# When the summed weight blocks of a pair are formed, and where the fourth sum is put

## Chip, cores and metric

The kernel runs on one core of a Trainium2 chip, in float32. The metric is the device time of one execution in microseconds (us), as the median of several runs. PE is the matmul engine (TensorE), DVE is VectorE, ACT is ScalarE, POOL is GpSimd and SP is SyncE, which issues most DMAs here.

## What is computed

One layer of an encoder trunk for 512 tokens of width 1024:

```python
h = _rmsnorm(x, g_pre_mix)
q, k, v, g, u, sv, a_ret, a_sgu = jnp.split(h @ w_in, ...)
y_ret = _retention_branch(q, k, v, g, ret_decay_logit, w_ret_o)
y_sgu = _sgu_branch(u, sv, sgu_ln_g, sgu_ln_b, w_spatial, b_spatial, w_sgu_o)
merged = jax.nn.sigmoid(a_ret) * y_ret + jax.nn.sigmoid(a_sgu) * y_sgu
x = x + _rmsnorm(merged @ w_out, g_post_mix)
h2 = _rmsnorm(x, g_pre_ffn)
x = x + _rmsnorm(_conv_gated_mlp(h2, w_up, conv_w, conv_b, w_down), g_post_ffn)
```

Nearly all of the time goes into the matrix products with w_in, w_ret_o, w_sgu_o, w_out, w_up and w_down.

## The kernel before

Every float32 operand of a product is split in two parts, hi (rounded, by ACT, line 79) and lo (the rest, by DVE, line 86), and a product is three matmuls: hi by hi, hi by lo, lo by hi.

Part of the products is done by Strassen's scheme in Winograd's form, with seven block products in place of eight. In the projections of u, of the two gates and in most of the up projection, 256 output columns form a *pair* (in the up projection, where two neighbouring tiles of the hidden layer are paired, it is called a couple here). Its weights are four blocks B11, B12, B21, B22 of 128 x 512 each, which come in two loads: a holds B11 and B12, b holds B22 and B21. Seven weight blocks, the *forms*, are wanted in the order B11, B21, T1, T2, T3, T4, B22, where

```python
T1 = B11 + B12;  T2 = T1 + B22;  T3 = B12 + B22;  T4 = T2 + B21
```

There are 20 pairs: four for u, four for each of the two gates, eight couples in the up projection. In the gates and the up projection two ordinary blocks of 128 x 1024 (`w_block`) stand between the forms of a pair, one after T2 and one after B22.

`w_form` makes one form: where needed it loads or adds, and then it splits the block into a slot of tag w4 (nine slots), from which PE reads. `w_get` calls it some units ahead of PE's use. The loads and the sums lie in tiles of tag raw, of which there are four buffers; a pair needs three of them: a, b, and t for the sums. T1 and T3 are added by DVE (lines 167 and 168), T2 and T4 by POOL (lines 169 and 171). T3 overwrites B12 in a; T2 is in the second half of t, and T4 overwrites T2.

The products of a pair are in the class `Pair`. Three PSUM tiles are in use. The product of T2 is copied out by ACT (line 79, `c<-ps` in the up projection) before the product of T3 is accumulated on the same bank; that of T3 is copied out in the same way before the second product of the activations with T4; and DVE's subtraction in line 720 reads the bank of T1's product before that of B22 is accumulated on it. Ordinary products (`f_block`) stand between.

A scheduler puts the instructions of each engine into an order when the program is built. It goes by the order in the source, by the free buffers and by its own estimate of times, so an instruction that is issued earlier in the source can bring others to other places. Each engine then runs its own list strictly in that order and waits at the head of it for semaphores of the others. POOL's list also has the DMAs that POOL issues, among them four loads of xT (line 658) in the middle of the first pair.

Of the kernel before, what the change touches and what calls it, by code (L numbers as in the profile page):

```python
# [13 lines left out]
ALU = mybir.AluOpType  # L14
# [3 lines left out]
S = 512  # L18
# [29 lines left out]
def tile_block(ctx: ExitStack, tc, xT, x, wall, par, cs, wsp, bsp, gpost, gffn, out):  # L48
    nc = tc.nc
# [6 lines left out]
    def nm(s):  # L56
        uid[0] += 1
        return f"{s}_{uid[0]}"

    def blk(dt=F32, n="blk", shape=(P, S)):  # L60
        return sb.tile(list(shape), dt, tag="blk", bufs=NBLK, name=nm(n))

    def tmp(n="tmp", shape=(P, S)):
        return sb.tile(list(shape), F32, tag="tmp", bufs=6, name=nm(n))
# [19 lines left out]
    def split(hi, lo, src):  # L84
        copy(hi, src)
        nc.vector.tensor_sub(lo, src, as32(hi))  # L86
# [31 lines left out]
    w_ready, w_pos, w_held, w_raw = {}, [0, 0], [0], {}  # L118

    def raw_tile():  # L120
        return sb.tile([P, 1024], F32, tag="raw", bufs=4, name=nm("raw"))
# [4 lines left out]
    def slot(n, at=0, w=1024):  # L126
        return sb.tile([P, 1088], F32R, tag="w4", bufs=9, name=nm(n))[:, at : at + w]
# [28 lines left out]
    def w_form(form, i):  # L156

        if form == "B11":
            a, b = raw_tile(), raw_tile()
            nc.sync.dma_start(a, wall[i])  # L160
            nc.sync.dma_start(b, wall[i + 1])
            w_raw["B11"], w_raw["B12"] = a[:, :S], a[:, S:]
            w_raw["B22"], w_raw["B21"] = b[:, :S], b[:, S:]
        elif form == "T1":
            t = raw_tile()
            w_raw["T1"], w_raw["T2"], w_raw["T3"], w_raw["T4"] = t[:, :S], t[:, S:], w_raw["B12"], t[:, S:]
            nc.vector.tensor_add(w_raw["T1"], w_raw["B11"], w_raw["B12"])  # L167
            nc.vector.tensor_add(w_raw["T3"], w_raw["B12"], w_raw["B22"])
            nc.gpsimd.tensor_tensor(out=w_raw["T2"], in0=w_raw["T1"], in1=w_raw["B22"], op=ALU.add)  # L169
        elif form == "T4":  # L170
            nc.gpsimd.tensor_tensor(out=w_raw["T4"], in0=w_raw["T2"], in1=w_raw["B21"], op=ALU.add)
        w = slot("wf", 0, 1088)
        lo, hi = w[:, AT_64 : AT_64 + S], w[:, S + AT_192 : 2 * S + AT_192]
        split(hi, lo, w_raw[form])
        return hi, lo
# [21 lines left out]
    def w_unit(u):  # L197
        return w_block(u[1]) if u[0] == "blk" else (w_down if u[0] in "qt" else w_form)(*u)
# [93 lines left out]
    T0, T1 = slice(0, 256), slice(256, 512)  # L292
# [35 lines left out]
    for t in range(NT):  # L328
        for n in range(2):
# [3 lines left out]
                out=xt, in_=xt, func=AF.Square, accum_out=ss[:, 4 * n + t : 4 * n + t + 1]  # L333
# [19 lines left out]
    for c in range(19, 1, -2):  # L353
        v.scalar_tensor_tensor(
            out=lc, in0=lc, scalar=1.0 / c, in1=lb, op0=ALU.add, op1=ALU.mult
# [4 lines left out]
        out=lg, in0=lc, scalar=-2.0, in1=lg, op0=ALU.mult, op1=ALU.add  # L360
# [5 lines left out]
    for m in range(8):  # L366
        t = blk(n="qkraw")
# [286 lines left out]
    for n, acc in enumerate(t_group()):  # L654
        if n < 2:
            for k in (n + 2, n + 6):
                t = tmp("xT")
# [663 lines left out]
```

## Time and profile before

| | |
|---|---|
| time, median of 3 runs | 827.69 us (824.78 to 828.19) |
| the profiled execution: its own time / its span | 827.49 us / 825.7 us |
| PE busy | 815.4 us (99%) |
| DVE busy | 661.4 us (80%) |
| ACT busy | 440.8 us (53%) |
| POOL busy | 101.0 us (12%) |
| POOL's T2 (line 169) | 20 times, mean 1.809 us |
| POOL's T4 (line 171) | 20 times, mean 1.333 us |
| granted clock of PE | 0.999 |

All lines quoted from the profile are of one execution. Times in the timeline are in us from the start of the span; a row gives start, duration, engine, line, operation, written tile <- read tiles, shapes and count, and in brackets how long the engine had been idle before it and what ended that. Rows of the groups give busy time and the mean of one in ns, then the idle time before them. Rows of the waits give the waiting instruction, the one waited for, the total, the count and the longest. Matmuls are pipelined, so their rows overlap: what one costs is the distance of its start to the next one's.

### The profile page before, as it was taken

The page shows a single profiled execution, that of the slowest core. Times are in us where ns is not written, and L with a number is a line of the kernel's source. Part 1 is how long each engine was busy: PE and PEld are TensorE (multiplying, and loading weights), DVE is VectorE, ACT ScalarE, POOL GpSimd, SP SyncE. Part 2 cuts the span into 40 slices and gives each one's busy share as a digit, 9 for nine tenths or more (in the row PEclk, how much of TensorE's full clock was granted, in tenths as well). Part 3 has the DMA queues.
Part 4 walks back from the last instruction along what each step waited for, and adds up shares of the span by engine and source line. Part 5 has one row for each costly group of instructions (what it writes and reads, how often), then busy time and mean ns, then how long its engine had stood idle before and what let it go on. Part 6 is the DMA issues. An engine that isn't in the chain of part 4 may idle for free.

```text
span 825.7 us, 13263 instructions
## 1 busy us (share of the span) xinstructions
PE 815.4 (99%) x5152; PEld 735.0 (89%) x5152; DVE 661.4 (80%) x1101; ACT 440.8 (53%) x771; POOL 101.0 (12%) x102
## 2 busy tenths in 40 slices
PE   9999999999999999999999999999999999999996
PEld 7888888888899999999988898899999998999996
DVE  7489897878797777767765568979899899988967
ACT  6636445546665444444445685556566566544531
POOL 0010000102121111132211211210111200000001
PEclk9999999999999999999999999999999999999999
DMA  8733222212223232222349111322322341233244
GB/s 294 246 116 102 77 77 77 77 52 78 90 102 129 103 102 80 101 101 103 108 166 339 48 55 55 103 102 103 102 103 102 102 154 52 77 115 129 96 147 154
DMA packets 29215, 93.24 MB, mean 113 GB/s; under 512 B 3360, under 2 KB 4000, under 8 KB 29152
## 3 DMA queue, kind: packets, MB, share of 16 engines
q1 hardware_dynamic: 26928, 86.85, 30.2%
q0 software_dynamic: 1360, 4.46, 1.6%
q10 hardware_dynamic: 864, 1.09, 0.4%
q8 instruction: 40, 0.66, 0.3%
q14 instruction: 23, 0.19, 0.1%
HBM read 88.19 MB, written 4.19 MB: 112 GB/s over the span
## 4 chain that ended last, share of the span: by engine, by line
PE 91%; DVE 6%; ACT 1%; issue 1%; DMA 0%; POOL 0%; DVEq 0%; SPq 0%; POOLq 0%; ACTq 0%
PE ps L692 23%; PE ps L217 12%; PE ps L218 12%; PE ps L219 12%; PE ps L1058 8%; PE ps L481 5%; PE ps L480 5%; PE ps L482 5%; PE ps L836 2%; PE ps L837 2%; PE ps L838 2%; PE ps L1074 1%; PE ps L761 1%; DVE fl L86 1%; PE ps L279 1%
## 5 line engine op out<-in xcount | busy, mean ns | idle before, releaser
L86 DVE TENSOR_TENSOR wl<-raw,wh 128x1024 fp32r<-128x1024 f32 (+1 forms) x93 | 109.1, 1182 | 48.9 <-PE ps L692 24.2
L79 ACT ACTIVATE wf<-raw 128x512 fp32r<-128x512 f32 x140 | 85.3, 627 | 102.7 <-PE ps L218 34.0
L86 DVE TENSOR_TENSOR wf<-raw,wf 128x512 fp32r<-128x512 f32 x140 | 111.1, 808 | 23.3 <-ACT wf L79 22.4
L692 PE MATMUL ps<-sh,wf 128*128 128x256 f32 x640 | 119.5, 277 | 0.0
L79 ACT ACTIVATE wh<-raw 128x1024 fp32r<-128x1024 f32 (+2 forms) x95 | 93.3, 993 | 37.4 <-DMA raw<-wall 17.0
L692 PEld LDWEIGHTS ps<-sh,wf 128*128 128x128 f32 x640 | 101.1, 188 | 0.8 <-ACT u L79 0.2
L217 PE MATMUL ps<-h2h,wh 128*128 128x512 f32 (+1 forms) x256 | 92.4, 363 | 0.7 <-ACT h2h L906 0.7
L218 PE MATMUL ps<-h2l,wh 128*128 128x512 f32 (+1 forms) x256 | 92.4, 363 | 0.0
L219 PE MATMUL ps<-h2h,wl 128*128 128x512 f32 (+1 forms) x256 | 92.1, 361 | 0.0
L692 PE MATMUL ps<-sl,wf 128*128 128x256 f32 x320 | 88.8, 278 | 0.0
L480 PE MATMUL ps<-wh,xh 128*128 128x512 f32 x192 | 75.0, 391 | 0.0
L481 PE MATMUL ps<-wl,xh 128*128 128x512 f32 x192 | 74.9, 390 | 0.0
L482 PE MATMUL ps<-wh,xl 128*128 128x512 f32 x192 | 74.8, 390 | 0.0
L169 POOL TENSOR_TENSOR raw<-raw,raw 128x512 f32<-128x512 f32 x20 | 36.2, 1809 | 235.2 <-DVE raw L167 207.8
L1058 PE MATMUL ps<-dl,fh 128*128 128x256 f32 x216 | 60.8, 281 | 0.1
L1058 PE MATMUL ps<-dh,fl 128*128 128x256 f32 x216 | 60.7, 281 | 0.0
L1058 PE MATMUL ps<-dh,fh 128*128 128x256 f32 x216 | 60.7, 281 | 0.0
L692 PEld LDWEIGHTS ps<-sl,wf 128*128 128x128 f32 x320 | 60.0, 188 | 0.6
L219 PEld LDWEIGHTS ps<-h2h,wl 128*128 128x128 f32 x256 | 48.0, 188 | 7.7
L217 PEld LDWEIGHTS ps<-h2h,wh 128*128 128x128 f32 x256 | 47.9, 188 | 7.9 <-ACT h2h L906 1.0
L692 PE MATMUL ps<-xh,wf 128*128 128x256 f32 x288 | 54.2, 278 | 0.0
L218 PEld LDWEIGHTS ps<-h2l,wh 128*128 128x128 f32 x256 | 48.0, 188 | 6.6
(314 smaller groups left out, 2048.9 us busy)
## 6 DMA issues: line engine op xcount, KB each, us to landing
raw<-wall SPq DMA_DIRECT2D x145, 512.0 KB, 3.6
x<-x SPq DMA_DIRECT2D x24, 256.0 KB, 5.9
xT<-xT SPq DMA_DIRECT2D x8, 256.0 KB, 5.4
x<-x POOLq DMA_DIRECT2D x8, 256.0 KB, 2.4
xT<-xT POOLq DMA_DIRECT2D x4, 256.0 KB, 3.6
out<-zg SPq DMA_DIRECT2D x4, 256.0 KB, 2.0
out<-zs ACTq DMA_DIRECT2D x3, 256.0 KB, 3.5
cs<-cs SPq DMA_DIRECT2D x2, 256.0 KB, 4.1
```

The lines of the kernel that those rows point to most:

```text
L79: nc.scalar.activation(out=o, in_=i, func=AF.Copy)
L86: nc.vector.tensor_sub(lo, src, as32(hi))
L169: nc.gpsimd.tensor_tensor(out=w_raw["T2"], in0=w_raw["T1"], in1=w_raw["B22"], op=ALU.add)
L217: nc.tensor.matmul(o, ah, bh, start=start, stop=False)
L218: nc.tensor.matmul(o, ah, bl, start=False, stop=False)
L219: nc.tensor.matmul(o, al, bh, start=False, stop=stop)
L480: nc.tensor.matmul(acc[t], xh[k][:, c], wh[:, f], start=k == 0, stop=False)
L481: nc.tensor.matmul(acc[t], xh[k][:, c], wl[:, f], start=False, stop=False)
L482: nc.tensor.matmul(acc[t], xl[k][:, c], wh[:, f], start=False, stop=k == KD - 1)
L692: nc.tensor.matmul(o, w_[:, c], a_, start=first and k == n == 0, stop=k == 3 and n == 2, skip_group_check=True,)
L836: nc.tensor.matmul(o, ah, bh, start=k == 0, stop=False)
L1058: nc.tensor.matmul(o, a_[:, c], w_[:, f], start=j == t == i == 0, stop=j == DP - 1 and i == 2 and n not in (M2, M3, M4), skip_group_check= ...
```

## The change

T1 and T2 are made as part of the pair's first form (B11), right after its two loads are issued, and t is taken there. T3 is made when it is its turn. T4 is made with form T1, and written over B11, so it no longer has to wait for the split of T2; in place of that it may not be written before B11 has been split.

```diff
             w_raw["B11"], w_raw["B12"] = a[:, :S], a[:, S:]
             w_raw["B22"], w_raw["B21"] = b[:, :S], b[:, S:]
+            t = raw_tile()
+            w_raw["T1"], w_raw["T2"], w_raw["T3"], w_raw["T4"] = t[:, :S], t[:, S:], w_raw["B12"], w_raw["B11"]
+            nc.vector.tensor_add(w_raw["T1"], w_raw["B11"], w_raw["B12"])
+            nc.gpsimd.tensor_tensor(out=w_raw["T2"], in0=w_raw["T1"], in1=w_raw["B22"], op=ALU.add)
+        elif form == "T3":
+            nc.vector.tensor_add(w_raw["T3"], w_raw["B12"], w_raw["B22"])
         elif form == "T1":
-            t = raw_tile()
-            w_raw["T1"], w_raw["T2"], w_raw["T3"], w_raw["T4"] = t[:, :S], t[:, S:], w_raw["B12"], t[:, S:]
-            nc.vector.tensor_add(w_raw["T1"], w_raw["B11"], w_raw["B12"])
-            nc.vector.tensor_add(w_raw["T3"], w_raw["B12"], w_raw["B22"])
-            nc.gpsimd.tensor_tensor(out=w_raw["T2"], in0=w_raw["T1"], in1=w_raw["B22"], op=ALU.add)
-        elif form == "T4":
             nc.gpsimd.tensor_tensor(out=w_raw["T4"], in0=w_raw["T2"], in1=w_raw["B21"], op=ALU.add)
```

## The prediction

> **What bounds the kernel now.** I read the page first, for the engines' shares, then the stretches of 20 us, for where TensorE (PE) has any time free, then who waited for whom on PE.
>
> ```profile
> span 825.7 us, 13263 instructions
> PE 815.4 (99%) x5152; PEld 735.0 (89%) x5152; DVE 661.4 (80%) x1101; ACT 440.8 (53%) x771; POOL 101.0 (12%) x102
> 180.00:200.00 20.00, 19.73 (x95) 16.11 (x94) 15.25 (x27) 12.04 (x20) 5.28 (x7) 1.00 0.25 80
> 200.00:220.00 20.00, 19.72 (x111) 16.91 (x110) 16.73 (x26) 12.19 (x22) 3.79 (x3) 1.00 0.20 66
> 560.00:580.00 20.00, 20.00 (x131) 18.15 (x130) 19.35 (x31) 13.28 (x23) 2.94 (x2) 1.00 0.28 102
> PE ps L605 <- DVE o L615: 0.3, 1, 0.3
> PE ps L624 <- DVE o L615: 0.3, 1, 0.3
> ```
>
> The first two lines say that the span is PE's work: 815.4 of 825.7 us, so 10.3 us is all that PE leaves, ends included. The three stretches (columns: length, PE, its weight loads, DVE, ACT, POOL, clock, DMA) lie where the 20 pairs of weights are formed; PE is free for 0.27 and 0.28 us in the first two and not at all in the third. PE's waits in that part are the last two lines, and neither names a sum of weights. In the changed program PE's instructions come in the same order, one for one. So the change can give back at most some tenths of a microsecond, and it can cost only where it makes PE wait.
>
> **What leaves, comes and moves.** No arithmetic is added: per pair two adds on DVE (T1, T3) and two on GpSimd (POOL: T2, T4), as before; no DMA is added and SP's queue keeps its order. Lines are those of before: T1 L167, T3 L168, T2 L169, T4 L171.
>
> ```profile
> L169 POOL TENSOR_TENSOR raw<-raw,raw 128x512 f32<-128x512 f32 x20 | 36.2, 1809 | 235.2 <-DVE raw L167 207.8
> POOL raw L171 <- DVE wf L86: 71.4, 19, 14.1
> 571.83 1.29 DVE L86 TENSOR_TENSOR wf<-raw,wf 128x512 fp32r<-128x512 f32 x2
> 573.03 0.69 DVE L86 TENSOR_TENSOR fl<-gp,fh 128x512 fp32r<-128x512 f32 x1
> 573.64 0.68 DVE L167 TENSOR_TENSOR raw<-raw 128x512 f32<-128x512 f32 x1
> 574.36 0.69 DVE L168 TENSOR_TENSOR raw<-raw,raw 128x512 f32<-128x512 f32 x1
> 574.97 0.42 DVE L720 TENSOR_TENSOR c<-ps,c 128x256 f32<-128x256 f32 x1
> 575.30 2.28 DVE L86 TENSOR_TENSOR wf<-raw,wf 128x512 fp32r<-128x512 f32 x2
> 574.55 1.64 POOL L169 TENSOR_TENSOR raw<-raw,raw 128x512 f32<-128x512 f32 x1 [19.45 <-DVE raw L167]
> 577.66 1.30 POOL L171 TENSOR_TENSOR raw<-raw,raw 128x512 f32<-128x512 f32 x1 [1.47 <-DVE wf L86]
> ```
>
> *The wait of T4.* POOL's T4 waited 71.4 us in 19 pairs for T2's split on DVE. That wait goes: T4 now needs T2, which POOL itself has just made, and the splits of B11, which are two products older. It is off PE's path: POOL has 12% of the span to do. What becomes late next is nothing on POOL; T2 and T4 now run back to back, about 1.64 + 1.30 = 2.9 us.
>
> *What that does to DVE.* At 574.55 T2 runs on POOL; the splits that DVE starts at 575.30 take 2.28 us for two, where the two at 571.83 take 1.29: 1.0 us is lost while POOL works. L720 in between, with one input from PSUM, keeps its 0.42. So each POOL sum that falls into a dense run of DVE costs DVE about 1.0 us, and the T4 that used to run at 577.66 now falls into the same run as T2. The Trainium skill (SBUF — State Buffer, "Who interferes with whom") says that a VectorE instruction with two SBUF inputs and a GpSimd instruction that reads SBUF exclude each other for a whole instruction, whichever issued second waiting; the row agrees, and this rule speaks against putting T4 right behind T2.
>
> *Where it meets PE.* In three couples of the up projection (those at 571, 613 and 634 us) the changed program also sets other work back: ACT's copy of the product of T3 of the couple before (L79, c<-ps) now stands behind the hi parts of the new T1 and T2, and DVE's L720 behind their lo parts. PE's next products into the same banks wait for these two.
>
> ```profile
> 573.87 0.38 ACT L79 ACTIVATE c<-ps 128x256 f32<-128x256 f32 x1 [1.29 <-PE ps L692]
> 576.23 0.63 ACT L79 ACTIVATE wf<-raw 128x512 fp32r<-128x512 f32 x1 [1.24 <-POOL raw L169]
> 576.42 0.28 PE L692 MATMUL ps<-h2h,wf 128*128 128x256 f32 x1
> 577.78 0.28 PE L692 MATMUL ps<-sh,wf 128*128 128x256 f32 x1
> 612.83 1.29 DVE L86 TENSOR_TENSOR wf<-raw,wf 128x512 fp32r<-128x512 f32 x2
> 618.78 0.28 PE L692 MATMUL ps<-sh,wf 128*128 128x256 f32 x1
> 634.02 1.29 DVE L86 TENSOR_TENSOR wf<-raw,wf 128x512 fp32r<-128x512 f32 x2
> 637.17 0.42 DVE L720 TENSOR_TENSOR c<-ps,c 128x256 f32<-128x256 f32 x1
> 639.28 0.28 PE L692 MATMUL ps<-sh,wf 128*128 128x256 f32 x1
> ```
>
> The copy is due before PE's 576.42, L720 before PE's 577.78. New order on DVE from 571.83: T1, B11 lo, an fl split, B21 lo, T1 lo, T2 lo, L720. Steps are 0.60 us apart (571.83 to 573.03 for two). T1 is done at about 572.5, T2 on POOL at 572.5 + 1.64 = 574.2, its hi part on ACT (0.63) at 574.9, the copy (0.38) at 575.3: 1.1 us early, hidden. L720 starts six steps on, 571.83 + 3.6 = 575.4, plus 1.0 us each for T2 and T4: 577.4, and is done at 577.9. PE is ready at 577.78, so it waits 0.1 us; with 1.1 us a sum, 0.3. I take 0.2. The couple at 613 us has the same order and the same distance (612.83 to 618.78, as 571.83 to 577.78, 5.95 us): 0.2 again. The third is later to begin with: 634.02 + 3.6 + 2.0 + 0.42 = 640.0 against 639.28, 0.75 us, of which the 0.4 that PE has lost by then is free if DVE does not slip with it. I take 0.6. Together +1.0.
>
> The other five couples keep their order, with T2 some 1.2 us earlier (T1 is now made ahead of the two splits of B11 and B21), which pays for T4's 1.0. One of them gains:
>
> ```profile
> 534.24 0.63 ACT L79 ACTIVATE wf<-raw 128x512 fp32r<-128x512 f32 x1 [1.19 <-POOL raw L169]
> 534.78 0.37 ACT L79 ACTIVATE c<-ps 128x256 f32<-128x256 f32 x1
> 534.62 0.39 PE L218 MATMUL ps<-h2l,wh 128*128 128x512 f32 x1
> 534.85 0.39 PE L219 MATMUL ps<-h2h,wl 128*128 128x512 f32 x1
> 535.20 0.39 PE L692 MATMUL ps<-h2h,wf 128*128 128x256 f32 x1
> 535.42 0.28 PE L692 MATMUL ps<-h2l,wf 128*128 128x256 f32 x1
> ```
>
> Here ACT's hi part of T2 waits 1.19 us for POOL and holds up the copy, which ends at 535.15; PE's step is 0.35 us in place of 0.23. The next step, with half the columns, is 0.22 in place of 0.12. With T2 earlier both go: -0.2 us.
>
> *The first twelve pairs.* Their margins are wide; the narrowest I found is the B11 of the pair used at 253.74:
>
> ```profile
> 247.65 1.78 DVE L86 TENSOR_TENSOR wf<-raw,wf 128x512 fp32r<-128x512 f32 x1
> 253.74 0.28 PE L692 MATMUL ps<-xh,wf 128*128 128x256 f32 x1
> 199.87 1.33 ACT L255 ACTIVATE xg<-xT,part 128x512 f32<-128x512 f32 x2
> 191.93 0.68 DVE L86 TENSOR_TENSOR wf<-raw,wf 128x512 fp32r<-128x512 f32 x1
> xT<-xT POOLq DMA_DIRECT2D x4, 256.0 KB, 3.6
> ```
>
> Its split ends at 249.4, 4.3 us before PE wants it; T4's 1.0 fits in. On POOL's queue the last of four loads of xT now stands behind the first T4, which waits for the B11 split that ends at 192.6. The load leaves at about 192.6 + 1.3 = 193.9, lands 3.6 later at 197.5, and is read by the second of the two copies that start at 199.87: hidden by over 2 us. Buffers: T2's place is free after T2's split instead of after T4's, B11's later, after T4's; the next pair's second load waits for the former and goes out earlier, so no load is late.
>
> **Sum.** +1.0 - 0.2 = +0.8 us on the profiled execution's 827.49 us, 828.3; the median of the runs is 827.69, so the forecast for the median lies at 828.4.
>
> **Rivals.** (a) *All of it is hidden.* If DVE loses less to POOL than 1.0 us a sum, or L720 slips in before the second hold, only the gain of 0.2 is left: 827.3 to 827.5. For it: margins of microseconds everywhere else. Against it: two sums now fall in one run. Chance 0.25. (b) *POOL is starved, and ACT's copy is late in every couple.* POOL does not always win:
>
> ```profile
> 510.93 3.42 POOL L169 TENSOR_TENSOR raw<-raw,raw 128x512 f32<-128x512 f32 x1 [27.27 <-DVE raw L167]
> 511.31 0.69 DVE L1012 TENSOR_TENSOR h<-h,xs 128x512 f32<-128x512 f32 x1
> 512.51 0.69 DVE L168 TENSOR_TENSOR raw<-raw,raw 128x512 f32<-128x512 f32 x1
> ```
>
> There T2 took 3.42 us while DVE's run went on undisturbed. In the couple at 571 us this puts T2's end at 572.5 + 3.42 = 575.9, its hi part at 576.6, the copy at 577.0 against 576.42: PE loses 0.6 us, and it decides from a T2 of about 2.8 us on. In all eight couples that is +4.8, and 832.3 or more. Against it: at 575.30 and at 247.65 it is DVE's split that is held up, and in five couples the copy already stood behind T2, which now starts earlier. Chance 0.13. By the skill's rule named above, POOL's sum, issued at 510.93, would have held L1012 back; the row shows otherwise, so the measurement decides. (c) *Faster by more than 0.5%* would need 4 us; the free time of PE shown above, 0.27 + 0.28 with the 0.2 at 535, is 0.8 us, 826.7. Only a difference between builds that I do not see gives more. Chance 0.05. The forecast's own case has the other 0.57.
>
> **Numbers.** 0.5%, 4.1 us, is about what a measurement of this kernel can tell from no change; three runs already spread from 824.78 to 828.19. Faster 0.05; slower 0.14 (case b and a little of the forecast's, if the three stalls each are over 1 us); the same 0.81. The range starts at 825.5, the hidden case less about 2 us for the lower of the runs, and ends at 831.5, which leaves out most of (b) and the faster case.
>
> **What would show it.** Right: T4 starting within 0.1 us of T2's end in nearly all pairs; T4's 71.4 us wait for DVE gone; DVE splits of 1.4 to 1.8 us twice in a row in the couples; L720 at about 577.5 and PE steps of 0.2 to 0.9 us too long at 577.8, 618.8 and 639.3; the step at 535 back at 0.23. Wrong: a T2 of over 2.8 us in several couples with ACT's copies behind it, waits of PE for a wf tile in the first twelve pairs, or a time outside 825.5 to 831.5.

## The result, and the profile after

The changed kernel takes 829.29 us (median of nine runs, 826.94 to 831.54) and the kernel before, run beside it, 824.78 us (nine runs, 823.28 to 828.19). The ratio of the two sets of runs is 1.0047 with a 95% interval of 1.0031 to 1.0062: 3.9 us slower, between 2.6 and 5.1 (the two medians alone lie 4.5 us apart). The profiled execution took 831.54 us, 4.05 more than the one before. The median fell into the range that was predicted and 0.9 us from the number, but by luck: the median of before that the prediction started from, 827.69 us of three runs, lay above the 824.78 of the nine. The right measure is the change itself: +0.8 was forecast and +3.9 came. That is 0.47%, just under the half per cent that the prediction took for what can be told from no change, and the interval reaches past it.

The head of the page and two of its groups, of the changed kernel:

```profile
span 829.8 us, 13300 instructions
PE 816.6 (98%) x5152; PEld 735.1 (89%) x5152; DVE 660.7 (80%) x1101; ACT 439.1 (53%) x771; POOL 116.3 (14%) x102
L167 POOL TENSOR_TENSOR raw<-raw,raw 128x512 f32<-128x512 f32 x20 | 51.5, 2576 | 270.7 <-DVE raw L166 127.0
L86 DVE TENSOR_TENSOR wf<-raw,wf 128x512 fp32r<-128x512 f32 x140 | 107.1, 781 | 29.0 <-ACT wf L79 28.9
```

PE has the same 5152 matmuls. DVE is not busier (660.7 us, before 661.4). What grew is POOL: T2, now line 167, takes 2576 ns in the mean, where it took 1809. The waits say who paid for that (waiting line, line waited for, total, count, longest); the last row here is of the kernel before:

```profile
PE ps L692 <- ACT c L79: 3.3, 4, 1.8
POOL raw L171 <- DVE wf L86: 6.9, 4, 2.6
ACT wf L79 <- POOL raw L167: 13.9, 4, 5.3
ACT wf L79 <- POOL raw L169: 9.5, 7, 2.9
```

The first line is new. Four times PE waits for ACT's copy of a product, 3.3 us in all. In the third line ACT waits for T2, four times, for 2.9 us and in the first couple of the up projection for 5.3. ACT waited for T2 before, too (last line: seven times, up to 2.9 us), and no wait of PE for a copy came of it, so ACT's wait alone is not the loss. T4's wait for DVE, 71.4 us before, is down to 6.9, as forecast; PE gains little by it.

PE's lists are the same one for one, so the start of the same matmul in both traces gives the delay at any place. Six such starts from the timeline of PE, after:

```profile
252.28 0.28 PE L692 MATMUL ps<-xh,wf 128*128 128x256 f32 x1
522.13 0.28 PE L692 MATMUL ps<-sh,wf 128*128 128x256 f32 x1
536.84 0.28 PE L692 MATMUL ps<-h2h,wf 128*128 128x256 f32 x1
579.95 0.28 PE L692 MATMUL ps<-sh,wf 128*128 128x256 f32 x1
621.97 0.28 PE L692 MATMUL ps<-sh,wf 128*128 128x256 f32 x1
643.28 0.28 PE L692 MATMUL ps<-sh,wf 128*128 128x256 f32 x1
```

Before, they stood at 253.74, 524.02, 535.20, 577.78, 618.78 and 639.28 us; all but the second are in the prediction's fences, and that one is the first of the two in this row of before:

```profile
524.02 0.39 PE L692 MATMUL ps<-sh,wf 128*128 128x256 f32 x2
```

The differences are -1.46, -1.89, +1.64, +2.17, +3.19 and +4.00. So the changed kernel was *ahead* until 522 us, by a matter of pace that is not the change's (last section). It then lost 3.65 us in the first couple of the up projection, of which 0.34 came back between 535 and 538 us, and 0.74, 1.11 and 0.81 us in the couples at 571, 613 and 634 us (by starts between the rows shown). From there to the end the difference stays at 4.08. These losses are larger than the waits beside them, since a wait counts only the time in which PE has nothing in flight; what counts is the distance between the starts.

**The couple at 571 us**, from the timeline of the changed kernel:

```profile
573.25 0.68 DVE L166 TENSOR_TENSOR raw<-raw 128x512 f32<-128x512 f32 x1
573.86 0.68 DVE L86 TENSOR_TENSOR wf<-raw,wf 128x512 fp32r<-128x512 f32 x1
575.06 1.28 DVE L86 TENSOR_TENSOR wf<-raw,wf 128x512 fp32r<-128x512 f32 x2
578.18 1.22 DVE L86 TENSOR_TENSOR wf<-raw,wf 128x512 fp32r<-128x512 f32 x1 [1.84 <-ACT wf L79]
579.32 0.41 DVE L720 TENSOR_TENSOR c<-ps,c 128x256 f32<-128x256 f32 x1
574.17 3.32 POOL L167 TENSOR_TENSOR raw<-raw,raw 128x512 f32<-128x512 f32 x1 [19.28 <-ACT fh L79]
577.57 1.29 POOL L171 TENSOR_TENSOR raw<-raw,raw 128x512 f32<-128x512 f32 x1
577.52 0.63 ACT L79 ACTIVATE wf<-raw 128x512 fp32r<-128x512 f32 x1 [2.85 <-POOL raw L167]
578.06 0.37 ACT L79 ACTIVATE c<-ps 128x256 f32<-128x256 f32 x1
578.48 0.38 PE L692 MATMUL ps<-h2h,wf 128*128 128x256 f32 x1 [0.48 <-ACT c L79]
```

POOL's T2 starts at 574.17 and takes 3.32 us in place of 1.64: DVE's splits at 573.86 and 575.06 keep their 0.68 and 1.28, so it is POOL that stands aside. (T4, right behind T2, does hold a split of DVE up: the one at 578.18 takes 1.22 us in place of 0.68.) ACT has T2's hi part at the head of its list and waits 2.85 us, with the copy behind it; the copy ends at 578.43 and PE starts at 578.48. L720 is done at 579.73, ahead of PE's 579.95: it is not what PE waits for.

**The first couple**, same view:

```profile
505.22 0.68 DVE L86 TENSOR_TENSOR sl<-h,sh 128x512 fp32r<-128x512 f32 x1
509.44 0.68 DVE L1012 TENSOR_TENSOR h<-h,xs 128x512 f32<-128x512 f32 x1
505.43 5.83 POOL L167 TENSOR_TENSOR raw<-raw,raw 128x512 f32<-128x512 f32 x1 [23.66 <-DVE raw L166]
511.30 0.63 ACT L79 ACTIVATE wf<-raw 128x512 fp32r<-128x512 f32 x1 [5.33 <-POOL raw L167]
512.48 0.70 DVE L86 TENSOR_TENSOR sl<-xs,sh 128x512 fp32r<-128x512 f32 x1 [2.37 <-ACT sh L79]
520.80 0.69 DVE L169 TENSOR_TENSOR raw<-raw,raw 128x512 f32<-128x512 f32 x1
521.52 1.15 ACT L79 ACTIVATE wf<-raw 128x512 fp32r<-128x512 f32 x2 [2.35 <-DVE raw L169]
523.76 0.37 ACT L79 ACTIVATE c<-ps 128x256 f32<-128x256 f32 x1
524.18 0.39 PE L692 MATMUL ps<-sh,wf 128*128 128x256 f32 x1 [1.77 <-ACT c L79]
```

T2 is held for as long as DVE runs without a gap (eight instructions from 505.22 to 510.12, of which the first and the last are shown) and takes 5.83 us. ACT waits 5.33 us, DVE then 2.37 us for ACT's next result, and everything behind comes later. DVE reaches T3 (line 169), which the change moved to the form of its own, at 520.80; ACT waits for it with the copy behind; PE is idle from 522.41 to 524.18. The granted clock then adds to it. The windows of that place (length, PE, weight loads, DVE, ACT, POOL, granted clock, DMA share, GB/s):

```profile
524.00:525.00 1.00, 0.82 (x6) 0.82 (x7) 1.00 (x2) 1.00 (x3) 0.00 (x0) 0.93 0.04 12
525.00:526.00 1.00, 1.00 (x7) 1.00 (x6) 1.00 (x3) 0.59 (x2) 0.00 (x0) 0.50 0.74 262
527.00:528.00 1.00, 1.00 (x4) 0.79 (x3) 1.00 (x2) 1.00 (x2) 0.00 (x0) 0.50 0.03 8
```

After the idle time the granted clock was 0.50 for three microseconds. By matched starts the delay grew by 1.6 us from 524.2 to 530 us with no wait in it. Of the nine runs five have a mean clock of 0.995 as in this profile (median 829.63 us) and four 0.997 to 0.998 (827.9 us); so this 1.6 us is probably not in all of them.

### The profile page after: what moved, and what is told of

It is laid out like the page before. It is cut to its first block, busy times and chain, and to the rows that moved or that the text cites. A ratio compares the mean times of both kernels' runs of the same rounds, so it can differ in the third digit from the quotient of the medians.

```text
span 829.8 us, 13300 instructions
## 1 busy us (share of the span) xinstructions
PE 816.6 (98%) x5152; PEld 735.1 (89%) x5152; DVE 660.7 (80%) x1101; ACT 439.1 (53%) x771; POOL 116.3 (14%) x102
## 4 chain that ended last, share of the span: by engine, by line
PE 82%; DVE 11%; ACT 2%; POOL 2%; issue 2%; DVEq 0%; POOLq 0%; ACTq 0%
PE ps L692 21%; PE ps L217 10%; PE ps L218 10%; PE ps L219 10%; PE ps L1058 8%; PE ps L480 5%; PE ps L481 5%; PE ps L482 5%; POOL raw L167 2%; PE ps L838 2%; PE ps L837 2%; PE ps L836 2%; DVE fl L86 1%; PE ps L1074 1%; DVE wl L86 1%
## 5 line engine op out<-in xcount | busy, mean ns | idle before, releaser
L86 DVE TENSOR_TENSOR wf<-raw,wf 128x512 fp32r<-128x512 f32 x140 | 107.1, 781 | 29.0 <-ACT wf L79 28.9
L167 POOL TENSOR_TENSOR raw<-raw,raw 128x512 f32<-128x512 f32 x20 | 51.5, 2576 | 270.7 <-DVE raw L166 127.0
```

## The experiments

The theory after the two traces: T2, made early, falls into a dense run of DVE (instructions one right behind the other), POOL is starved, ACT's copy behind T2's hi part is late. The rivals: T4 right behind T2 does it (the prediction's own reason), T3's new place does it, or the early sums of the first twelve pairs do. In the expectations, theory A is the first form of this (the order on ACT and DVE costs), A2 the later one (ACT's wait for the starved T2, and PE behind it); rival B is the two POOL sums back to back, rival C the order on ACT alone. In the text below *added* is the delay that PE collects between the matched matmuls at 521 and 645 us of before, against the trace of before; it is 5.97 us for the changed kernel, 4.4 without the half clock.

**T3 back beside T1** (against the changed kernel; T3 is made with T4 in form T1):

```diff
-        elif form == "T3":
-            nc.vector.tensor_add(w_raw["T3"], w_raw["B12"], w_raw["B22"])
         elif form == "T1":
+            nc.vector.tensor_add(w_raw["T3"], w_raw["B12"], w_raw["B22"])
```

> The changed kernel, but with DVE's sum T3 made with form T1 again. Theory A (what costs is the order on ACT and DVE: in the first couple of the up projection a late T3 holds up ACT and with it the copy PE waits for, and in three later couples the copy stands behind T2): the wait of 1.8 us near 522 us and the slow clock after it go, 3.3 us in all, the three waits of 0.5 to 0.8 us near 578, 620 and 641 us stay; 1.5 to 2.5 us above the kernel before. Rival B (two GpSimd sums back to back cost, by the port shared with DVE): as the changed kernel, 4 us above before.

Measured 827.89 us against 826.34, ratio 1.0027 (1.0013 to 1.0042); added 4.83 us. The four waits remain. The first couple's falls from 1.77 to 0.54 us, without a slow clock after it; the three later couples lose 1.4 to 1.5 each, more than with T3 late and more than expected, since T3 now lies in the same run of DVE and T2 takes 3.92 us there. So T3's late place costs in the first couple and saves some in the three later ones.

**T4's place alone** (against before; T1, T2, T3 as they were):

```diff
-  ... w_raw["T4"] = t[:, :S], t[:, S:], w_raw["B12"], t[:, S:]
+  ... w_raw["T4"] = t[:, :S], t[:, S:], w_raw["B12"], w_raw["B11"]
             ...
             nc.gpsimd.tensor_tensor(out=w_raw["T2"], ...)
-        elif form == "T4":
             nc.gpsimd.tensor_tensor(out=w_raw["T4"], ...)
```

> The kernel before, with one part of the change: T4 is written over B11 and made with form T1, right behind T2; T1, T2 and T3 are made where they were. The order on ACT stays that of before. Theory A: within 1 us of the kernel before, no new wait of PE, DVE holds of 1.0 us hidden. Rival B: 2 us or more above before, PE waiting for copies or for L720 in the couples.

Measured 825.23 us, ratio 0.9986 (0.9972 to 1.0000); added -0.35 us. PE has no wait for a copy. The timeline of POOL in the couple at 571 us:

```profile
574.55 1.64 POOL L169 TENSOR_TENSOR raw<-raw,raw 128x512 f32<-128x512 f32 x1 [20.98 <-DVE raw L167]
576.27 1.63 POOL L170 TENSOR_TENSOR raw<-raw,raw 128x512 f32<-128x512 f32 x1
```

T2 and T4 run back to back, as in the changed kernel, and cost nothing; the late steps from 535 to 538 us are gone, 0.35 us. The rival that blamed T4 behind T2 falls.

**T3's place alone** (against before):

```diff
-            nc.vector.tensor_add(w_raw["T3"], w_raw["B12"], w_raw["B22"])
             nc.gpsimd.tensor_tensor(out=w_raw["T2"], ...)
+        elif form == "T3":
+            nc.vector.tensor_add(w_raw["T3"], w_raw["B12"], w_raw["B22"])
```

> The kernel before, with T3 alone moved to its own form; T1, T2 and T4 as before. Theory A: only the first couple of the up projection can suffer, where T3 now comes late on DVE and ACT's hi part of T3 and the copies wait for it; since ACT is not held by an early T2 there, less than in the changed kernel, 0 to 2 us; the later couples keep their times. If the late T3 alone is the whole cause, 3.3 us. Rival B: as before, within 1 us.

Measured 826.15 us, ratio 1.0002 (0.9987 to 1.0018); added 1.27 us. There is one wait, in the first couple. Its timeline on DVE, ACT and PE:

```profile
522.72 0.68 DVE L170 TENSOR_TENSOR raw<-raw,raw 128x512 f32<-128x512 f32 x1
523.42 1.15 ACT L79 ACTIVATE wf<-raw 128x512 fp32r<-128x512 f32 x2 [2.35 <-DVE raw L170]
526.09 0.39 PE L693 MATMUL ps<-sh,wf 128*128 128x256 f32 x1 [1.28 <-ACT c L79]
```

It is the chain of the first couple with an undisturbed T2: T3 late on DVE, ACT waits 2.35 us for it, PE 1.28 us for the copy. This 1.28 and the 0.54 that T3 back beside T1 leaves make 1.82, near the changed kernel's 1.77. The ratio alone could not have told that from nothing; the trace does.

**T1 and T2 early, the rest as before** (against before; T3 stays in form T1, T4 in form T4 and over T2):

```diff
             w_raw["B22"], w_raw["B21"] = b[:, :S], b[:, S:]
-        elif form == "T1":
             t = raw_tile()
             ...
             nc.vector.tensor_add(w_raw["T1"], ...)
-            nc.vector.tensor_add(w_raw["T3"], ...)
             nc.gpsimd.tensor_tensor(out=w_raw["T2"], ...)
+        elif form == "T1":
+            nc.vector.tensor_add(w_raw["T3"], ...)
```

> The kernel before, with the other part: T1 and T2 are made with the first form; T3 stays with form T1, T4 with its own form over T2. On ACT the copy stands behind T2's hi part in three couples, as in the changed kernel. Theory A: three waits of PE of 0.5 to 0.8 us near 578, 620 and 641 us, T2 taking about 3.3 us there, no wait near 522; 1.5 to 2.5 us above before. Rival B: as the kernel before, within 1 us.

Measured 829.75 us, ratio 1.0037 (1.0023 to 1.0051); added 4.91 us. This half of the change makes a loss as large by itself, and more than expected: PE waits 1.0 to 1.1 us in each of the three later couples and 0.56 in the first. The couple at 571 us on POOL, ACT and PE:

```profile
573.92 3.92 POOL L167 TENSOR_TENSOR raw<-raw,raw 128x512 f32<-128x512 f32 x1 [17.64 <-ACT fh L79]
577.88 0.63 ACT L79 ACTIVATE wf<-raw 128x512 fp32r<-128x512 f32 x1 [3.46 <-POOL raw L167]
578.84 0.39 PE L692 MATMUL ps<-h2h,wf 128*128 128x256 f32 x1 [1.07 <-ACT c L79]
```

With T3 in the same dense run of DVE, T2 takes 0.6 us longer than in the changed kernel (3.92 and 3.32), and PE's wait is 0.6 us longer (1.07 and 0.48). Between these two kernels the length of T2 goes one for one into PE's wait.

**T4 at its own form again** (against the changed kernel):

```diff
-  ... w_raw["T4"] = t[:, :S], t[:, S:], w_raw["B12"], w_raw["B11"]
+  ... w_raw["T4"] = t[:, :S], t[:, S:], w_raw["B12"], t[:, S:]
             ...
-        elif form == "T1":
+        elif form == "T4":
             nc.gpsimd.tensor_tensor(out=w_raw["T4"], ...)
```

> The changed kernel without the move of T4: T1 and T2 early, T3 with its own form, T4 over T2 with its own form as before. Theory A2: T4's place has no part in the loss: as the changed kernel, 3 to 5 us above before, PE waiting 1.3 to 1.8 us near 522 and 0.5 to 1.1 us in three couples. Rival B (two GpSimd sums back to back): 2 us below the changed kernel.

Measured 829.85 us against 825.03, ratio 1.0066 (1.0044 to 1.0089); added 5.35 us. The waits of PE for a copy are four, 4.3 us. Taking T4 away from T2's back helps nothing.

**T2 on DVE** (against the changed kernel):

```diff
-            nc.gpsimd.tensor_tensor(out=w_raw["T2"], in0=w_raw["T1"], in1=w_raw["B22"], op=ALU.add)
+            nc.vector.tensor_add(w_raw["T2"], w_raw["T1"], w_raw["B22"])
```

> The changed kernel with T2 added by DVE instead of GpSimd. Theory A2: ACT no longer waits 2.8 us for T2 in the couples, PE's waits for copies go; DVE has 0.6 us more work a pair, which is hidden where it idles; within 1.5 us of before, 2.5 us or more below the changed kernel. Rival C: PE's waits stay at 0.5 us or more. If DVE is the bound, the time rises by up to 20 x 0.6 = 12 us above before.

Measured 824.14 us against 825.03, ratio 0.9983 (0.9967 to 0.9999); added -0.35 us, and no wait for a copy. The scheduler also put the copy ahead of T2's hi part here, so this run takes away both the slow sum and its place before the copy. What it does show is that 20 more adds on DVE are free, and that T4 on POOL may be slow without harm:

```profile
573.81 0.38 ACT L79 ACTIVATE c<-ps 128x256 f32<-128x256 f32 x1 [0.64 <-PE ps L692]
574.48 2.74 POOL L171 TENSOR_TENSOR raw<-raw,raw 128x512 f32<-128x512 f32 x1 [21.84 <-DVE raw L167]
```

**No sum for T2 in the couples** (against the kernel with T1 and T2 early; T1's block is split a second time in its place, so this kernel leaves a sum out and does not compute the layer; by the names of their tiles the lists of ACT and DVE are the same one for one, with the copy still behind the two hi parts):

```diff
-            nc.gpsimd.tensor_tensor(out=w_raw["T2"], ...)
+            if i < UP0:
+                nc.gpsimd.tensor_tensor(out=w_raw["T2"], ...)
+            else:
+                w_raw["T2"] = w_raw["T1"]
```

> The kernel with T1 and T2 made early (T3 and T4 as before), but in the eight couples of the up projection the sum T2 is left out: T2's form is split from T1, and T4 adds to T1. The lists of ACT keep the copy behind the hi parts of T1 and T2. Theory A2 (the wait for a GpSimd sum that DVE's dense run starves is what holds ACT and so PE): no wait of PE for a copy at 578, 620 and 641 us, at most 0.5 us near 522; within 1 us of before. Rival C (the order on ACT alone costs, two splits ahead of the copy): the waits stay at 0.5 us or more, 1.5 to 2.5 us above before.

Measured 824.10 us, ratio 0.9997 (0.9982 to 1.0013); added -0.35 us: all four waits are gone. In the couple at 571 us, on ACT and POOL:

```profile
571.33 1.15 ACT L79 ACTIVATE wf<-raw 128x512 fp32r<-128x512 f32 x2
572.59 0.39 ACT L79 ACTIVATE c<-ps 128x256 f32<-128x256 f32 x1
571.46 4.53 POOL L174 TENSOR_TENSOR raw<-raw,raw 128x512 f32<-128x512 f32 x1 [20.66 <-ACT fh L79]
```

The two hi parts run without a wait, and the copy, still behind them, is early. T4 has slipped into the dense run and takes 4.53 us, but nobody waits for it; in the first couple it takes even 10.05 us. So it is not a slow POOL that costs, but a slow POOL with ACT's copy queued behind its result.

**The early sums in the first twelve pairs only** (against the kernel with T3 back beside T1; `early_sums` makes T1 and T2 as the two removed lines did; the couples call it in form T1, the twelve pairs in form B11):

```diff
-            nc.vector.tensor_add(w_raw["T1"], ...)
-            nc.gpsimd.tensor_tensor(out=w_raw["T2"], ...)
+            if i < UP0:
+                early_sums()
         elif form == "T1":
+            if i >= UP0:
+                early_sums()
```

> T1 and T2 made with the first form only in the twelve pairs ahead of the up projection; in the couples with form T1. T3 with form T1 and T4 over B11 in all pairs. Theory A2: nothing of the loss is left, PE waits for no copy; as the kernel with T4 alone moved, 1 us below before, within 1 us. If the early sums cost in the first twelve pairs too: 1.5 us or more above that.

Measured 822.90 us against 825.03, ratio 0.9985 (0.9969 to 1.0001); added -0.35 us, with no wait for a copy. The twelve pairs lie ahead of the stretch where the delay is added; from 180 to 521 us the delay against before grows nowhere by more than 0.03 us from one matmul to the next, here and in the changed kernel. So the first twelve pairs hide the early sums, as forecast. Its interval, that of T4's place alone and that of T2 on DVE end at 1.0001, 1.0000 and 0.9999: all three lie below the changed kernel's, and whether one beats the kernel before is on the edge of what was measured.

**All together.** The lowest run of each kernel, less the lowest run of before in the same set, follows the added delay of the profiled executions:

| kernel | added, us | lowest run less before's, us |
|---|---|---|
| changed | 5.97 (4.4 without the half clock) | +3.7 |
| T3 back beside T1 | 4.83 | +4.3 |
| T1, T2 early | 4.91 | +5.3 |
| T4 at its own form | 5.35 | +4.9 |
| T3's place alone | 1.27 | +1.0 |
| T4's place alone | -0.35 | -0.3 |
| T2 on DVE | -0.35 | -0.9 |
| no T2 in the couples | -0.35 | -0.1 |
| early in the first twelve | -0.35 | -1.1 |

Four couples hold the change's whole effect. The measured ratios lie up to 2.2 us from the last column, mostly below it, because the runs of each kernel spread by 3 to 5 us, probably for another reason (last section).

## Why the prediction was right or wrong

*PE bounds, its order stays, only waits can cost.* Right: the loss is PE's new waits and, in the profiled execution, 1.6 us of slow clock behind one of them.

*T4's wait goes, T2 and T4 back to back.* T4 starts 0.08 us behind T2 (574.17 + 3.32 = 577.49, and 577.57), and the wait of 71.4 us is 6.9. But "about 1.64 + 1.30 = 2.9 us" is 4.6 in that couple.

*"Each POOL sum that falls into a dense run of DVE costs DVE about 1.0 us."* Wrong, and the step that failed. One row of before, the splits of 2.28 us at 575.30, was taken for the rule; the row quoted with rival (b), 3.42 us at 510.93, had the other outcome, and that is what came for T2 in every couple: DVE's run stays at its pace and POOL pays, 5.83, 3.32 or 2.72 us for a sum that took about 1.65 in seven of the eight. T4 did hold a split up, by about 0.5 us at 578.18 in place of the 1.0.

*"The copy ... 1.1 us early, hidden."* Wrong by this failure: with T2 at 3.32 in place of 1.64 us, and T1 done at 573.93 by the changed trace's clock, the copy came 0.48 us late. "L720 0.2, 0.2 and 0.6 us late" had the place right and the cause wrong: PE does lose in these three couples, 0.74, 1.11 and 0.81 us, together 2.66 in place of 1.0, but behind the copy; L720 was in time at 571.

*"The other five couples keep their order."* This left out the largest term. In the first couple T2's 5.83 us and T3's later place together cost 1.9 us of waiting; the half clock, which no step had reckoned with, added 1.6. The step promised T3 no cost because it looked at T1 and T2 in that couple and not at T3, whose hi part stands before a copy too. The other four lost nothing.

*The gain at 535 us.* Right: the steps there are 0.23 and 0.12 us; with the next few it is -0.34 in place of -0.2.

*The first twelve pairs hidden.* Right, by the run that has the change in them alone.

*The rivals.* (b) named the mechanism, POOL starved and ACT's copy late from a T2 of about 2.8 us on, and gave it 0.13; it was wrong in the number of couples, four in place of eight, and did not see T3 or the clock. Its +4.8 lies inside the measured 2.6 to 5.1, and the forecast's +0.8 does not; the prediction's own sign of being wrong, a T2 of over 2.8 us in several couples with ACT's copies behind it, came. (a) is what T4's place alone does. The forecast was thus near the time by a sum whose largest term was missing and whose next one was 1.7 us too small, set on a start that lay 2.9 us above the median of the nine.

The rule drawn on was the Trainium skill's (SBUF — State Buffer, "Who interferes with whom"): whoever issues first holds the shared port for its instruction, the other waits. The exclusion is borne out, since POOL's sum takes 1.29 us alone and 5.83 beside eight of DVE's. That only the one instruction ahead would be waited for is not: POOL's T2, issued at 505.43, was passed by the seven that DVE issued after it.

## What to carry to other kernels

Before moving an operation to an earlier place, look at what the other engine on the shared port does there: a GpSimd sum inside a gapless run of two-input VectorE instructions can last as long as the run, as in the couples here. Then look at what stands behind its *consumer* in the consumer's list; it was a copy that had nothing to do with the sum that stopped PE. When one trace shows an arbitration going both ways, cost the change by both rows, in every place where it can fall, rather than by the one nearest.

## What was not expected of the hardware

*Two paces of the same matmuls.* Stretches of 128x256 matmuls run at about 0.113 or 0.118 us a step, differing between runs of the same list. The windows from 225 to 265 us and from 742 to 800 us, of before:

```profile
225.00:265.00 40.00, 40.00 (x328) 39.52 (x327) 37.04 (x57) 25.09 (x45) 10.34 (x7) 1.00 0.36 125
742.00:800.00 58.00, 58.00 (x495) 58.00 (x494) 47.51 (x78) 27.41 (x43) 0.54 (x1) 1.00 0.37 127
```

The same two of the changed kernel:

```profile
225.00:265.00 40.00, 40.00 (x335) 39.20 (x334) 38.66 (x58) 25.08 (x46) 12.11 (x8) 1.00 0.37 120
742.00:800.00 58.00, 58.00 (x495) 58.00 (x495) 48.51 (x80) 27.17 (x43) 0.54 (x1) 1.00 0.36 117
```

And the second of the kernel with T4's place alone:

```profile
742.00:800.00 58.00, 58.00 (x514) 58.00 (x514) 48.01 (x78) 27.99 (x44) 0.54 (x1) 1.00 0.39 132
```

The granted clock is 1.00 and PE is never idle, yet 328 or 335 matmuls fit into the first window, 495 or 514 into the second. This is the 1.9 us by which the changed kernel was ahead at 522, and some 3 us that the other kernels, like T4's place alone, gain on both of these after 645 us. It is likely also the spread of 823 to 828 us in the runs of before; that last was not shown, nor what sets the pace.

*Half the clock after a short stop.* PE idled 1.77 us, and 0.50 was granted from 525 to 528 us. The Trainium skill (TensorE: Matmul & The Clock Gate, Part 1) gives half rate as the idle state, reached after an idle window of about 3.4 us that runs free. The 0.50 agrees; that a stop must last 3.4 us does not, and the kernel with T4 at its own form waited 2.22 us at the same place with the clock at 1.00 throughout. Where the stop falls may matter. In the clock record of the changed kernel's trace the clock changes at 524.86, 528.27 and 825.23 us; the first two lie 3.413 us apart and the last 87 times that further on, so these changes lie on one grid. The whole 1.77 us (522.41 to 524.18) fell into one step of it, 521.45 to 524.86. In the other kernel's record the full clock ends at 823.86 us; counted back from there in the same steps, an edge at 523.49 cuts its stop (522.44 to 524.66) into 1.05 and 1.17 us. The idle share of one step would thus explain both; two stops do not prove it.

*Who wins the port* stays open too. POOL was passed over at 505.43 and 574.17, and in before it held DVE's splits up at 575.30, where line 720, with an input from PSUM, had just run on DVE. That such a gap in DVE's two-input run is what lets POOL in fits these rows, but not these of the changed kernel, in one of the first twelve pairs:

```profile
210.94 0.69 DVE L615 TENSOR_TENSOR o<-o,g 128x512 f32<-128x512 f32 x1
211.55 1.78 DVE L169 TENSOR_TENSOR raw<-raw,raw 128x512 f32<-128x512 f32 x1
211.18 1.61 POOL L167 TENSOR_TENSOR raw<-raw,raw 128x512 f32<-128x512 f32 x1 [16.64 <-DVE raw L166]
```

DVE's instructions follow each other here without a gap and read two inputs from SBUF, as at 505.43, and POOL comes in after one of them: DVE's T3 takes 1.78 us in place of 0.69.
